# Gram and low-rank matmuls of two heads issued alternately on TensorE, in a one-core hybrid RWKV-7 / S5 / RG-LRU layer

## The chip, the cores and the metric

The kernel runs on one core of one Trainium2 chip. The metric is the device time of one execution in microseconds (us). Engines are named as in the profile: PE is TensorE (PEld its weight loads), DVE is VectorE, ACT is ScalarE, POOL is GpSimd, SP is the engine that issues the DMAs.

## What is computed

One layer (DEPTH is 1, 2048 frames, model width 1024, all float32). The input is normalised and projected to 4224 columns; three groups of 512 columns (RWKV-7, S5, RG-LRU) are mixed in time, gated, projected back and added; then comes a gated per-layer embedding and a final norm. The change lies in the RWKV-7 group, whose recurrence per head of width 64 is:

```
z = z + mu * (z_prev - z)
r, k, v, wd, ad = jnp.split(z, [...])
w = -jax.nn.softplus(-(w0 + jnp.tanh(wd) @ w2)) - 0.5          # low-rank matmul 1
a = jax.nn.sigmoid(a0 + ad @ a2)                               # low-rank matmul 2
kk = heads(k * k_k); kk = kk / max(norm(kk), 1e-12)
k = k * (1.0 + (a - 1.0) * k_a); b_h = kk * a_h; decay = exp(-exp(w))
def step(S, inp):
    S = S * d_t - (S kk_t) b_t^T + v_t k_t^T
    return S, S r_t
```

The reference steps frame by frame. The kernel does it in chunks of 64 frames: within a chunk all products of (b, k) of one frame with (kk, r) of another are needed, weighted with the decays between them. These are the Gram matrices of a chunk and a head: a 128 x 128 product with a contraction over the head's 64 channels.

## The kernel before, in words

The program has three parts in time. The mixers run to about 1143 us: the input projection (function `fills`, matmuls of lines 332 to 334, 128x512, three for each of eight slices, since the float32 product is split in a high and a low part) interleaved with the RWKV-7 work. After them come S5 with an output projection, and at the end the gated embedding and the final norm. The change touches the first part only.

RWKV-7 work is cut into 16 units: two head pairs and 256 frames each. A head pair fills the 128 partitions, head h = 0 on partitions 0 to 63 and head h = 1 on 64 to 127; the 512 columns of a unit's tiles are two pairs by 256 frames, or 8 chunks of 64 (index c). Each unit passes three stages, which run beside each other for successive units:

- *front* (`rwkv_front`): the two low-rank matmuls (line 396 into the PSUM tile `ps`, from partitions 0 to 63 of `zl`; line 398 into `psa`, from partitions 64 to 127), one each for the unit's two head pairs `hp`; from `ps` come `s`, its running sum `psl` (line 404) and the decays `ep`, `einv`; from `psa` comes `ta`. Then `kx` (kk and r, times decay) and `bk` (b and k, over decay) are made. Last come the Gram matmuls (line 461), in two halves of four chunks (`half_c`). For each half and each head there are four matmuls, lhsT = `bk` and rhs = `kx`, both on that head's 64 partitions, into one PSUM tile of 512 columns. That tile is then read by two ACT copies into `mt` (line 466) and two DVE multiplications with a mask into `kx` and `gr` (line 468, shown by the profile as line 80, the helper).
- *solve* (`rwkv_solve`): DVE inverts 32 x 32 blocks taken from `mt`: a transpose into `ms` (line 478) and 31 steps of a multiply and a subtract (`stmp`, `xs`, lines 487 and 489); PE completes the 64 x 64 inverses (lines 530 and 541), makes the bonus sums (line 511 into `psq`, read by DVE into `bon`) and transposes keys and values.
- *chain* (`rwkv_chain`): the state goes from chunk to chunk, PE matmuls of lines 570 to 603 between small DVE and ACT steps.

The order on PE is written out: the loop at line 883 takes steps of the projections and of the three stages by a credit, counted in matmuls, and under `manual_schedule` PE keeps exactly that order. The order on DVE, ACT and of the DMA issues on SP is set by the scheduler of the framework, by priorities and its own estimate of when each instruction can run. So a change of PE's order can also move instructions on the other engines.

The PSUM tiles of the front are taken from a ring of two banks named `prep`:

```
def pprep():
    return psum.tile([P, 512], F32, tag="prep", name="ps_prep", bufs=2)
```

In order of the program the ring serves `ps`, `psa`, `psn` (line 418), then head 0 and head 1 of the first Gram half, head 0 and head 1 of the second, and `psq` of a solve in between; each waits until the last reader of the tile two places before is done.

Each of these float32 matmuls is two entries in the profile: the 256 Gram matmuls of the program are 512 PE entries of line 461.

## Time and profile before

| what | value |
|---|---|
| timed runs | 1842.55, 1842.67, 1846.06 us (median 1842.67) |
| span of the profiled execution | 1844.3 us (the profile gives no other time for it) |
| PE busy, whole span | 1758.3 us, 95% |
| DVE busy, whole span | 1316.9 us, 71% |
| ACT busy, whole span | 928.6 us, 50% |
| stretch 60 to 1143 us (mixers) | PE busy 1054.91 of 1083 us, DVE 823.38, ACT 647.31 |
| Gram matmuls, line 461 | 512 entries, 55.8 us busy, 284 ns mean |
| low-rank matmuls, lines 396 and 398 | 64 entries each, 18.0 and 18.9 us busy |
| granted PE clock | 0.986 of full speed over the span |

How to read it: busy time of PE adds up entries that may overlap, and the ends of matmuls are modelled, so what a block of matmuls costs is read from the start of its first entry to the start of the next block, not from the sum of durations. The chain of waits follows the work that ended last back through the program: at each step to what released an instruction, or to the one before it on its engine. Work that isn't on that chain can get faster without the end moving.

### The profile page before, as it was taken

What the parts mean: (1) busy time and instruction counts of PE and PEld (TensorE: products, weight loads), DVE (VectorE), ACT (ScalarE), POOL (GpSimd) and SP (SyncE); (2) the same over time, 40 slices, a digit from 0 to 9 for tenths busy, and PEclk for the clock granted to TensorE, in tenths of its full rate; (3) what the DMA queues carried; (4) which work ended last, traced back from release to release, by engine and by line L of the source; (5) the groups of instructions that cost most, each with busy time, mean ns of one, the idle gap of its engine ahead of it and who ended that gap; (6) DMA issues with size and microseconds to landing.
All of it is one profiled execution on the core that took longest, in us unless ns stands there. A gap on an engine that the chain in (4) does not pass through costs nothing.

```text
span 1844.3 us, 30269 instructions
## 1 busy us (share of the span) xinstructions
PE 1758.3 (95%) x11244; PEld 1355.6 (74%) x11244; DVE 1316.9 (71%) x3301; ACT 928.6 (50%) x1797; POOL 39.8 (2%) x101
## 2 busy tenths in 40 slices
PE   5999999999998999999999999799999999999997
PEld 4877777777676777677776677577778878888886
DVE  6279788787986349898787875789996674455444
ACT  5345864575757444765557657433442443222222
POOL 1000000000000000000000000000000000000000
PEclk9999999999999999999999999899999999999999
DMA  4332322222223232223222122743435992122110
GB/s 145 120 111 68 97 90 85 90 60 76 83 78 103 92 123 76 66 90 106 80 76 66 53 60 87 193 147 102 121 121 165 254 293 82 65 70 76 58 46 35
DMA packets 214621, 184.72 MB, mean 100 GB/s; under 512 B 59253, under 2 KB 182474, under 8 KB 214474
## 3 DMA queue, kind: packets, MB, share of 16 engines
q1 hardware_dynamic: 214474, 182.79, 32.6%
q8 instruction: 89, 1.46, 0.3%
q14 instruction: 58, 0.48, 0.1%
HBM read 121.73 MB, written 59.83 MB: 98 GB/s over the span
## 4 chain that ended last, share of the span: by engine, by line
PE 64%; DVE 21%; ACT 8%; issue 4%; DMA 2%; POOL 0%; SPq 0%; POOLq 0%; ACTq 0%; DVEq 0%
PE ps_mm L332 9%; PE ps_mm L333 8%; PE ps_mm L334 8%; PE ps_mm L924 7%; PE ps_mm L922 7%; PE ps_mm L923 7%; DVE xs L80 3%; DVE stmp L80 3%; PE ps_prep L461 2%; ACT L101 1%; DVE w L80 1%; DVE ms L478 1%; PE ps_prep L1208 1%; PE ps_chain L570 1%; PE ps_prep L319 1%
## 5 line engine op out<-in xcount | busy, mean ns | idle before, releaser
L332 PE MATMUL ps_mm<-xh,whi 128*128 128x512 f32 x1056 | 462.9, 438 | 0.9 <-ACT whi L192 0.7
L333 PE MATMUL ps_mm<-xh,wlo 128*128 128x512 f32 x1056 | 415.9, 394 | 0.8 <-DVE wlo L80 0.8
L334 PE MATMUL ps_mm<-xl,whi 128*128 128x512 f32 x1056 | 416.0, 394 | 0.0
L332 PEld LDWEIGHTS ps_mm<-xh,whi 128*128 128x128 f32 x1056 | 199.8, 189 | 79.0 <-issue 31.2
L333 PEld LDWEIGHTS ps_mm<-xh,wlo 128*128 128x128 f32 x1056 | 200.4, 190 | 46.8 <-issue 13.1
L334 PEld LDWEIGHTS ps_mm<-xl,whi 128*128 128x128 f32 x1056 | 199.7, 189 | 45.3
L922 PE MATMUL ps_mm<-woh,yh 128*128 128x512 f32 x256 | 103.6, 406 | 12.2 <-ACT yh L101 12.2
L80 DVE TENSOR_TENSOR stmp<-xs,ms 128x60 f32<-128x60 f32 (+24 forms) x496 | 103.6, 209 | 11.6
L80 DVE TENSOR_TENSOR xs<-xs,stmp 128x60 f32<-128x60 f32 (+24 forms) x496 | 102.9, 207 | 11.5
L98 DVE SCALAR_TENSOR_TENSOR e<-ftg,e 128x1024 f32<-128x1024 f32 x16 | 19.6, 1226 | 118.6 <-ACT ftg L101 118.6
L923 PE MATMUL ps_mm<-woh,yl 128*128 128x512 f32 x256 | 102.8, 402 | 0.2 <-DVE yl L98 0.2
L924 PE MATMUL ps_mm<-wol,yh 128*128 128x512 f32 x256 | 103.0, 402 | 0.0
L924 PE MATMUL ps_mm<-pgl,hh 128*128 128x512 f32 x256 | 101.0, 395 | 0.0
L923 PE MATMUL ps_mm<-pgh,hl 128*128 128x512 f32 x256 | 100.9, 394 | 0.0
L922 PE MATMUL ps_mm<-pgh,hh 128*128 128x512 f32 x256 | 100.8, 394 | 0.0
L80 DVE TENSOR_TENSOR wlo<-wraw,whi 128x512 fp32r<-128x512 f32 x132 | 88.5, 684 | 14.9 <-ACT whi L192 14.5
L101 ACT ACT_TABLE_LOAD x70 | 89.8, 1283 | 12.2 <-DVE cs L80 11.0
L101 ACT ACTIVATE ftg<-ps_mm 128x512 f32<-128x512 f32 x32 | 19.1, 598 | 136.7 <-PE ps_mm L924 136.7
L98 DVE SCALAR_TENSOR_TENSOR z<-ps_mm,pc,z 128x511 f32<-128x511 f32 x48 | 35.8, 745 | 68.9 <-ACT z L101 68.8
L192 ACT CAST whi<-wraw 128x512 fp32r<-128x512 f32 x132 | 77.9, 614 | 0.9 <-DMA wraw<-in_w_in 0.5
L101 ACT ACTIVATE uv<-ps_chain 64x128 f32<-64x128 f32 x64 | 17.4, 272 | 97.3 <-DVE uv L93 96.7
L101 ACT ACTIVATE z<-ps_mm,dc 128x512 f32<-128x512 f32 x48 | 32.8, 682 | 65.4 <-PE ps_mm L334 65.2
(331 smaller groups left out, 3554.8 us busy)
## 6 DMA issues: line engine op xcount, KB each, us to landing
wraw<-in_w_in SPq DMA_DIRECT2D x132, 256.0 KB
zd<-z SPq DMA_DIRECT2D x48, 256.0 KB
yr<-Yd SPq DMA_DIRECT2D x16, 512.0 KB
ht<-in_x SPq DMA_DIRECT2D x16, 512.0 KB
Hd<-ht SPq DMA_DIRECT2D x16, 512.0 KB
hr<-Hd SPq DMA_DIRECT2D x16, 512.0 KB
out<-e SPq DMA_DIRECT2D x16, 512.0 KB
st<-in_w_out SPq DMA_DIRECT2D x12, 512.0 KB
```

The source lines that it names most:

```text
L80: V.tensor_tensor(out=out, in0=a, in1=b, op=op)
L98: V.scalar_tensor_tensor(out=out, in0=a, scalar=s, in1=b, op0=op0, op1=op1)
L101: A.activation(out=out, in_=in_, func=func, scale=scale, bias=bias)
L192: A.copy(out=hi[:, ks], in_=raw)
L319: T.transpose(out=ps[:, q * P:(q + 1) * P], in_=row[q][k // 4][:, k % 4 * P:(k % 4 + 1) * P], identity=ident)
L332: T.matmul(out=ps, lhsT=hi[:, k], rhs=xh, start=(k == 0), stop=False)
L333: T.matmul(out=ps, lhsT=lo[:, k], rhs=xh, start=False, stop=False)
L334: T.matmul(out=ps, lhsT=hi[:, k], rhs=xl, start=False, stop=(k == KD - 1))
L461: T.matmul(out=ps[:, q * P:(q + 1) * P], lhsT=bk[hs, c].rearrange("p a t -> p (a t)"), rhs=kx[hs, c, h:3:2 - h], start=True, stop=True)
L922: T.matmul(out=ps, lhsT=a_h[:, k], rhs=b_h[k][:, ns], start=(k == 0), stop=False)
L923: T.matmul(out=ps, lhsT=a_l[:, k], rhs=b_h[k][:, ns], start=False, stop=False)
L924: T.matmul(out=ps, lhsT=a_h[:, k], rhs=b_l[k][:, ns], start=False, stop=(k == nk - 1))
```

## The change

The two heads' Gram matmuls of a half are issued in turn: chunk by chunk, first head 0, then head 1, each head still into a PSUM tile of its own. Both tiles are therefore taken from the ring before the first matmul, and the readers (ACT copies, DVE multiplications) of both heads stand behind all eight matmuls in the program. The two low-rank matmuls are issued in turn likewise, for each head pair one of each. The number of instructions, their operands and the PSUM tiles stay as they were. Comment lines are removed too, which shifts line numbers by one or so: in the changed kernel the low-rank matmuls are lines 396 and 397, the Gram matmul is line 460.

```diff
         for hp, cs in hps:
             T.matmul(out=ps[:, cs], lhsT=wla[0:64, hp * P:(hp + 1) * P], rhs=zl[0:64], start=True, stop=True)
-        for hp, cs in hps:
             T.matmul(out=psa[:, cs], lhsT=wla[64:128, hp * P:(hp + 1) * P], rhs=zl[64:128], start=True, stop=True)
...
         for half_c in range(2):
             yield 1
             cs = slice(4 * half_c, 4 * half_c + 4)
+            pair_ps = [pprep(), pprep()]
+
+            for q in range(4):
+                c = 4 * half_c + q
+                for h in range(2):
+                    hs = slice(64 * h, 64 * h + 64)
+                    T.matmul(out=pair_ps[h][:, q * P:(q + 1) * P], lhsT=bk[hs, c].rearrange("p a t -> p (a t)"),
+                             rhs=kx[hs, c, h:3:2 - h], start=True, stop=True)
             for h in range(2):
                 os = slice(64 * (1 - h), 64 * (1 - h) + 64)
-                ps = pprep()
-                for q in range(4):
-                    c = 4 * half_c + q
-                    hs = slice(64 * h, 64 * h + 64)
-                    T.matmul(out=ps[:, q * P:(q + 1) * P], lhsT=bk[hs, c].rearrange("p a t -> p (a t)"),
-                             rhs=kx[hs, c, h:3:2 - h], start=True, stop=True)
-                psq4 = ps.rearrange("p (c t) -> p c t", t=P)
+                psq4 = pair_ps[h].rearrange("p (c t) -> p c t", t=P)
                 for bl in range(2):
                     g = slice(64 * h + 32 * bl, 64 * h + 32 * bl + 32)
                     A.copy(out=mt[g, cs, 0:C - 32 * bl], in_=psq4[g, :, 32 * bl:C])
```

On PE, at the Gram matmuls of the first unit's first half: `ps_prep_1063` is head 0's PSUM tile, `ps_prep_1072` (before) and `ps_prep_1064` (after) head 1's; `x4` means four matmuls in a row. Before:

```order
L334 MATMUL ps_mm_1042<-xl_478,whi_867 128x512
L461 MATMUL ps_prep_1063<-kx_978,bk_988 128x128 x4
L461 MATMUL ps_prep_1072<-kx_978,bk_988 128x128 x4
L332 MATMUL ps_mm_1042<-xh_489,whi_867 128x512
L333 MATMUL ps_mm_1042<-xh_489,wlo_868 128x512
```

Now:

```order
L460 MATMUL ps_prep_1063<-kx_978,bk_988 128x128
L460 MATMUL ps_prep_1064<-kx_978,bk_988 128x128
L460 MATMUL ps_prep_1063<-kx_978,bk_988 128x128
L460 MATMUL ps_prep_1064<-kx_978,bk_988 128x128
L460 MATMUL ps_prep_1063<-kx_978,bk_988 128x128
L460 MATMUL ps_prep_1064<-kx_978,bk_988 128x128
L460 MATMUL ps_prep_1063<-kx_978,bk_988 128x128
L460 MATMUL ps_prep_1064<-kx_978,bk_988 128x128
```

The four of head 1 moved up between those of head 0; the projections around them stand as before. The same holds for all 32 such blocks.

On PE, at the low-rank matmuls of the first unit (`ps_prep_936` is `ps`, `ps_prep_937` is `psa`), before:

```order
L334 MATMUL ps_mm_915<-xl_466,whi_795 128x512
L396 MATMUL ps_prep_936<-zl_892,wla_242 128x256 x2
L398 MATMUL ps_prep_937<-zl_892,wla_242 128x256 x2
L332 MATMUL ps_mm_915<-xh_477,whi_795 128x512
L333 MATMUL ps_mm_915<-xh_477,wlo_796 128x512
```

Now:

```order
L396 MATMUL ps_prep_936<-zl_892,wla_242 128x256
L397 MATMUL ps_prep_937<-zl_892,wla_242 128x256
L396 MATMUL ps_prep_936<-zl_892,wla_242 128x256
L397 MATMUL ps_prep_937<-zl_892,wla_242 128x256
L332 MATMUL ps_mm_915<-xh_477,whi_795 128x512
```

The second head pair's matmul into `ps` now stands behind the first one into `psa`. Apart from these two kinds of block PE's order is the same from end to end.

On DVE the instructions are the same ones, but their order moved. At the eighth unit's running sum `psl`, which stands among the seventh unit's solve steps (`stmp`, `xs`) and chain steps (`sp`, `uv`), before:

```order
L80 TENSOR_TENSOR stmp<-xs,ms 128x2x27
L404 SCALAR_TENSOR_TENSOR psl<-cmask,s 128x512
L80 TENSOR_TENSOR xs<-xs,stmp 128x2x27
L80 TENSOR_TENSOR stmp<-xs,ms 128x2x26
L80 TENSOR_TENSOR xs<-xs,stmp 128x2x26
L98 SCALAR_TENSOR_TENSOR lth<-lr,lth 128x512
```

Now:

```order
L80 TENSOR_TENSOR xs<-xs,stmp 128x4x16
L80 TENSOR_TENSOR wlo<-wraw,whi 128x512
L80 TENSOR_TENSOR stmp<-xs,ms 128x5x15
L692 COPY lru_h<-lr 128x1
L403 SCALAR_TENSOR_TENSOR psl<-cmask,s 128x512
L80 TENSOR_TENSOR xs<-xs,stmp 128x5x15
```

`psl` moved back by 36 instructions, from the solve step of width 27 to that of width 15. It is the largest move on DVE: of its 3303 instructions 992 stand at another place than before, 798 of these by at most four places. ACT has 70 loads of function tables instead of 71.

## The prediction

> **What bounds the kernel now.** I read the page first, then the busy times by stretch, then the chain of waits, then single blocks on the timeline.

> ```profile
> span 1844.3 us, 30269 instructions
> PE 1758.3 (95%) x11244; PEld 1355.6 (74%) x11244; DVE 1316.9 (71%) x3301; ACT 928.6 (50%) x1797; POOL 39.8 (2%) x101
> PE 64%; DVE 21%; ACT 8%; issue 4%; DMA 2%; POOL 0%; SPq 0%; POOLq 0%; ACTq 0%; DVEq 0%
> 60.00:1143.00 1083.00, 1054.91 (x8099) 784.49 (x8098) 823.38 (x2392) 647.31 (x1313) 12.96 (x36) 0.99 0.28 83
> ```

> The third line is the chain's share by engine; the last is the mixers' stretch (length, then busy time of PE, PEld, DVE, ACT, POOL). PE is almost never idle there, 28 us of 1083, and looks like the bound. But DVE is busy for 823 us (76%), and a fifth of the chain is DVE's. So PE and DVE take turns in setting the end, and what PE saves counts only where the chain runs over PE. Everything that is changed lies in this stretch; the later 701 us stay.

> **What a Gram block costs.** One block (half a unit, both heads) on the PE timeline: start, time from the first start to the last end, line, shape, number of entries.

> ```profile
> 113.28 1.71 PE L461 MATMUL ps_prep<-kx,bk 64*128 64x128 f32 x16
> 114.92 0.50 PE L332 MATMUL ps_mm<-xh,whi 128*128 128x512 f32 x1
> ...
> 1057.26 1.16 PE L461 MATMUL ps_prep<-kx,bk 64*128 64x128 f32 x8
> 1060.94 1.13 PE L461 MATMUL ps_prep<-kx,bk 64*128 64x128 f32 x8 [2.53 <-DVE gr L80]
> ```

> The last two rows are lucky: in this one block head 1 had to wait for its PSUM bank, so each head stands alone. A head alone takes 1.16 or 1.13 us; both in a row take 1.71, not 2.3. So they overlap already, with head 1 starting about 1.71 - 1.16 = 0.55 us after head 0. If they started together the block would take 1.16 and a bit. Whether they can is shown by two other blocks, which have the wanted order or act like it:

> ```profile
> 99.25 0.48 PE L396 MATMUL ps_prep<-zl,wla 64*128 64x256 f32 x1
> 99.26 0.48 PE L398 MATMUL ps_prep<-zl,wla 64*128 64x256 f32 x1
> ...
> 100.00 0.38 PE L396 MATMUL ps_prep<-zl,wla 64*128 64x256 f32 x1
> 100.01 0.38 PE L398 MATMUL ps_prep<-zl,wla 64*128 64x256 f32 x1
> ...
> 129.72 1.15 PE L519 MATMUL ps_late<-cen,zv 64*64 64x64 f32 x32
> ...
> L519 PE MATMUL ps_late<-cen,zv 64*64 64x64 f32 x512 | 18.4, 221 | 0.7 <-ACT kb L506 0.7
> ```

> The low-rank matmuls of lines 396 and 398, on the two halves of the partitions as the Gram matmuls are, start 0.01 us apart from first to last, although all four entries of 396 stand ahead of those of 398 in the program. Line 519 alternates the heads already: 32 entries in 1.15 us, one of them 0.22 long (last row: the group's mean is 221 ns), so one every (1.15 - 0.22) / 31 = 0.03 us. PE can thus issue far faster than the 1.16 / 16 = 0.07 us that the alternated Gram block asks for, and a second stream on the other 64 partitions costs 0.01 us. My reading: PE looks ahead over a few entries only. Four of the other head are within reach (low rank), eight are not (Gram), and alternation puts the partner next in line.

> **The change, part by part.** *Gram.* New block: 1.16 + 0.01 = 1.17 us; saved 1.71 - 1.17 = 0.54 us per block. There are 512 entries / 16 = 32 blocks, so PE's own slots shrink by 32 x 0.54 = 17.3 us. The bounds of the saving per block are 0 (PE starts head 1 no earlier, for a reason that the rows don't show) and 0.55 (no offset at all); I take 0.54, since the low-rank pairs show it on the same row halves.

> *Low rank.* Worth 0 on PE where nothing waits: the pairs overlap to 0.01 us before. In a few units `psa` waits for its bank; the longest of these waits (the bracket is idle time and its releaser):

> ```profile
> 462.64 1.13 PE L396 MATMUL ps_prep<-zl,wla 64*128 64x256 f32 x4
> 465.26 2.04 PE L398 MATMUL ps_prep<-zl,wla 64*128 64x256 f32 x4 [1.50 <-DVE stmp L80]
> ```

> Head 1's rows start 2.62 us late here, for DVE has to free the bank. Now the second matmul into `ps` queues behind the waiting one, so `s` and the sum `psl` can start up to 2.6 us later than today. PE's own end stays: after the wait four entries of each stream run side by side at most, as four of 398 do today. The cover for the late `s` is the distance from here to the unit's Gram matmuls, which the chain's list puts at 512.67, 47 us later. So I cost it at 0; without that cover it would cost up to 2.6 us in this unit.

> *Readers.* The same ACT copies and DVE multiplications as before; head 0's results are ready at the same time after the block's start (1.16 us), head 1's 0.54 earlier. Nothing is added there. The wait that is new: head 1's bank is needed at the start of the block instead of 0.55 us into it, and all of head 0's matmuls but the first stand behind it.

> *What of 17.3 us lies on the chain.* The list of the longest pieces of the chain shows which Gram blocks set the end:

> ```profile
> 113.35 1.64 PE ps_prep L461 x16
> 157.79 1.85 PE ps_prep L461 x15
> 222.31 1.64 PE ps_prep L461 x16
> 226.63 1.10 PE ps_prep L461 x11
> ...
> 512.67 1.64 PE ps_prep L461 x16
> ...
> 682.67 1.89 PE ps_prep L461 x15
> ...
> 720.12 1.66 PE ps_prep L461 x15
> 724.84 1.78 PE ps_prep L461 x16
> ...
> 1003.47 1.64 PE ps_prep L461 x16
> 1007.76 1.10 PE ps_prep L461 x11
> 1060.94 1.13 PE ps_prep L461 x8
> ```

> Of 32 blocks, 28 are in it. Sixteen are whole and undisturbed (x16, 1.64 us; first 113.35, last 1003.47), and 720.12 is nearly that: 17 blocks. Seven (x11; first 226.63, last 1007.76) are left after 11 entries: the chain goes over to ACT when head 0 is ready, and head 0 gets no faster. Four (157.79, 682.67, 724.84, 1060.94) contain a wait for another engine. Four are off the chain. What follows an x11 block:

> ```profile
> 227.75 0.36 ACT mt L466
> ...
> 256.69 0.28 ACT uv L101
> ...
> 257.02 0.45 PE ps_chain L592 x8
> ```

> From 227.75 to 257.02 the end is set by ACT's copies, the solve on DVE and what DVE and ACT do between, and PE, busy all that time, joins again at line 592. If PE arrives there 0.54 us sooner, it waits 0.54 us longer. How close the two paths are is in the waits of PE in 60 to 1150 us (total, times, longest):

> ```profile
> PE ps_chain L592 <- ACT uv L101: 3.0, 6, 0.8
> ```

> Six waits of 0.8 us at most: the two paths have the same length within a microsecond. That is why I count the x11 and the off-chain blocks (11 x 0.54 = 5.9 us) at nothing. The four with waits I count at nothing as well; they are worth between 0 and 0.54 each.

> *Sum.* 17 x 0.54 = 9.2 us on the chain. Taking time off one path brings the other up at some of these 17 places too; I take 2 of them as lost (between 0 and 17; the six short waits say few), so 15 x 0.54 = 8.1 us. The profiled execution would go from 1844.3 to 1836.2. The median of the timed runs, 1842.7, lies 1.6 below that span, so I forecast 1842.7 - 8.1 = **1834.6 us**.

> *The reordered DVE and ACT.* The moves of 992 DVE instructions cost or gain what the trace of before can't show. A solve step is a pair of 0.2 us:

> ```profile
> L80 DVE TENSOR_TENSOR stmp<-xs,ms 128x60 f32<-128x60 f32 (+24 forms) x496 | 103.6, 209 | 11.6
> ```

> The largest move, 36 places, is worth at most about 36 x 0.2 = 7 us of delay for one `psl`, under the 47 us of cover; the moves of up to four places are worth 0.8 us each, with both signs. As a sum I take 0, with 4 us to either side (an estimate: five such moves that fall the same way and are met by a waiting PE). One load of a function table less on ACT is left at 0, ACT being busy for 647 of 1083 us.

> **The rivals.**

> *All of PE's saving counts (chance 0.17).* If DVE follows PE (its moved order lets the solves start sooner), all blocks but the four with waits pay: 28 x 0.54 = 15.1 us, 1827.6 us. For it: PE busy 97% of the stretch. Against it: the x11 blocks, and 29 us of DVE and ACT on end behind one of them.

> *The gain turns into waits for PSUM banks (chance 0.18).* Banks are freed by DVE, which isn't faster. Behind the second half of a unit the freeing stands late on DVE:

> ```profile
> 342.01 0.42 DVE L80 TENSOR_TENSOR gr<-ps_prep,gm 128x256 f32<-128x256 f32 x1
> 342.35 2.03 DVE L478 STREAM_TRANSPOSE ms<-mt 128x1024 f32<-128x1024 f32 x1
> ...
> 345.73 0.41 DVE L80 TENSOR_TENSOR gr<-ps_prep,gm 128x256 f32<-128x256 f32 x1
> ```

> Head 1's bank is free at 346.1, 3.7 us after head 0's at 342.4, because the transpose stands between. A PE that is ahead meets this at the next user of the ring, as it does today at 465.26. If it eats 12 or more of the 17, at most 5 x 0.54 = 2.7 us remain: 1840 to 1843, say 1841 us. Against it: at 222 to 227 and the like both halves run without a wait. [...]

> *Slower: DVE's new order makes PE wait (chance 0.10).* Chain steps (`sp`, `uv`) that now stand behind more solve steps come late, and PE, in written order, waits at line 592 in unit after unit. A move by four places costs 4 x 0.2 = 0.8 us; ten such waits that aren't there today (8.1 / 0.8) undo the forecast's gain, and from there on the time gets longer. With one in each of the 16 units it is 16 x 0.8 - 8.1 = 4.7 us slower, 1847.4 us. For it: DVE is 76% busy and a fifth of the chain. Against it: most moves are small and of both signs.

> *The change doesn't do what it says (chance 0.03).* If PE serialised entries whose partner has just started, blocks would stay at 1.71 and the time at 1842.7. The low-rank rows speak against it.

> **How the numbers follow.** Forecast 0.52, all counts 0.17, waits 0.18, no effect 0.03, slower 0.10. The likeliest case alone spans 1831 to 1839 (8.1 with 4 either way). The range takes in the full saving below and no saving above: 1827 to 1844; slower than 1844 and faster than 1827 together hold under 2 in 10. What a measurement of this kernel tells from no change is about 0.2%, 3.7 us, so faster means under 1839.0 and slower over 1846.4. Faster: all of the 0.17, 0.48 of the 0.52 and 0.05 of the waits, 0.70. Same: the forecast's edge (0.04), the rest of the waits and no effect (0.16), the mildest fifth of the slower case (0.02), 0.22. Slower: 0.08.

> **What would show it.** In the changed profile a Gram block of 16 entries reads 1.17 us instead of 1.71, with the next line-332 matmul 0.54 us sooner; if it reads 1.4 or more, the look-ahead step is wrong. Line 396 and its partner stay 0.01 us apart. PE's waits at 592 and 581 and for `prep` banks grow by some 6 to 9 us in total; if they grow by 15, the second rival holds, if by 2, the first. The mixers end (1143 us before) at about 1135; a move elsewhere, after 1143, would refute that the change works where I say.

## The result and the profile after

The change makes the kernel slower: 1859.58 us (median of four runs, 1856.73 to 1864.2) against 1843.05 (four runs, 1842.55 to 1846.06). The ratio is 1.0084, 95% interval 1.0066 to 1.0102. The forecast was 1834.6 with a range up to 1844, so sign and range are both wrong. One of the ten executions of run e7 (below) took 2446.71 us at a granted clock of 0.656; that run's median and ratio are of the other nine.

From the page of the changed kernel: span, busy times, the chain's share by engine; then the mixers' stretch from the busy times by stretch (length, PE, PEld, DVE, ACT, POOL busy, granted clock, DMA share and GB/s).

```profile
span 1862.5 us, 30258 instructions
PE 1758.8 (94%) x11244; PEld 1351.0 (73%) x11244; DVE 1321.6 (71%) x3301; ACT 928.0 (50%) x1796; POOL 39.9 (2%) x101
PE 56%; DVE 25%; ACT 10%; issue 4%; DMA 3%; POOL 0%; SPq 0%; POOLq 0%; ACTq 0%; DVEq 0%
60.00:1143.00 1083.00, 1035.48 (x7950) 765.57 (x7949) 816.65 (x2369) 630.75 (x1287) 13.05 (x36) 0.97 0.27 82
```

PE, DVE and ACT are less busy in this stretch, and fewer of their instructions fall into it (7950 of PE's entries instead of 8099). On the chain PE's share fell from 64% to 56%, and DVE's and ACT's together rose from 29% to 35%. PE's granted clock in the stretch fell from 0.99 to 0.97.

All of the loss lies in the mixers. The last `ps_y` matmuls of the mixers (line 603 before, 604 after; start, time, shape, entries), first before, then after:

```profile
1142.38 0.40 PE L603 MATMUL ps_y<-gr,uv 128*64 128x64 f32 x8
```

```profile
1162.04 0.40 PE L604 MATMUL ps_y<-gr,uv 128*64 128x64 f32 x8
```

The mixers end 19.66 us later; the span grew by 18.2. Yet the Gram block did get shorter, as wanted (timeline of PE, after):

```profile
224.44 1.16 PE L460 MATMUL ps_prep<-kx,bk 64*128 64x128 f32 x16
225.53 0.50 PE L332 MATMUL ps_mm<-xh,whi 128*128 128x512 f32 x1
```

From the block's start to the next line-332 matmul it is 1.09 us, where the undisturbed block of before at 113.28 has 114.92 - 113.28 = 1.64. What grew are PE's waits (after; 60 to 1170 us; total, times, longest):

```profile
PE ps_prep L460 <- DVE gr L80: 8.5, 4, 4.2
PE ps_prep L512 <- ACT nrow L419: 5.5, 1, 5.5
...
PE ps_prep L460 <- DVE bk L80: 5.2, 3, 2.4
PE ps_chain L593 <- ACT uv L101: 4.2, 7, 0.8
...
PE ps_prep L397 <- DVE stmp L80: 2.4, 1, 2.4
```

All of PE's rows of this view up to 1165 us add up to 47.1 us after and 27.6 before. The new ones are few and long.

**Where the time went.** PE runs the same `ps_y` matmuls in the same order in all kernels, so their starts can be subtracted. The table gives, for eleven of the 64 groups of line 603, how much later (+) each kernel starts them than the kernel before. All are taken from the timelines of PE, one profiled execution of each kernel; the runs are described below. The executions differ: that of e3 is the slowest of its ten (1852.74, median 1845.67), those of before and after are the slowest of four, that of e9 is the fastest of four. So a step counts here where several columns show it.

| start before, us | after | e5 | e9 | e10 | e6 | e3 | e2 | e1 | e4 | e7 |
|---|---|---|---|---|---|---|---|---|---|---|
| 257.30 | 1.5 | 0.9 | 0.7 | 1.1 | 0.4 | 1.1 | 0.6 | 0.8 | -1.3 | -1.2 |
| 371.28 | 3.4 | 5.5 | 3.7 | 1.2 | 0.4 | 1.1 | 1.9 | -0.4 | -1.2 | 1.6 |
| 402.58 | 8.5 | 5.5 | 3.7 | 1.2 | 0.4 | 7.4 | 8.0 | -0.5 | -1.8 | 1.6 |
| 472.85 | 5.7 | 3.9 | 2.0 | -0.1 | 0.3 | 4.7 | 2.7 | -2.6 | -8.7 | -4.8 |
| 497.74 | 12.2 | 11.0 | 8.9 | 1.8 | 0.4 | 4.6 | 4.4 | -2.6 | -9.2 | -5.7 |
| 611.68 | 11.9 | 10.3 | 8.2 | 1.2 | 2.4 | 4.5 | 4.8 | -3.2 | -7.7 | -4.8 |
| 738.31 | 14.9 | 13.5 | 11.4 | 2.9 | 0.8 | 7.9 | 5.9 | -4.8 | -9.1 | -2.9 |
| 784.96 | 14.1 | 12.5 | 10.4 | 2.0 | 0.9 | 7.4 | 5.1 | -4.8 | -9.1 | 1.3 |
| 796.67 | 18.6 | 14.8 | 12.7 | 2.0 | 0.9 | 7.4 | 5.1 | -4.8 | -5.8 | 1.3 |
| 926.84 | 16.6 | 14.6 | 12.5 | 2.1 | 0.9 | 4.6 | 4.2 | -5.5 | -7.9 | 2.7 |
| 1142.38 | 19.7 | 14.4 | 14.0 | 5.0 | 0.9 | 5.9 | 6.2 | -2.9 | -10.7 | 1.5 |

The kernel after loses in a few steps: 5.1 us between 371 and 403, 6.5 between 473 and 498, 3.0 between 612 and 738, 4.5 between 785 and 797. In between the figure falls, by 0.55 us at an undisturbed Gram block and where the kernel before loses time itself, as at 465 us. Two of the steps were followed down to their cause. In each of the other two PE waits at a Gram block for DVE's `bk` (2.44 us at 733.44, 2.06 us at 801.51); why `bk` is late there stays open.

**The step at 473 to 498 us: the running sum comes late.** After, on ACT, DVE and PE:

```profile
472.84 0.84 ACT L101 ACTIVATE s<-ps_prep,dc 128x256 f32<-128x256 f32 x2
...
482.25 0.62 ACT L101 ACTIVATE s<-s 128x512 f32<-128x512 f32 x1
...
486.00 1.22 DVE L403 TENSOR_TENSOR_SCAN psl<-cmask,s 128x512 f32<-128x512 f32 x1
...
487.25 0.63 ACT L101 ACTIVATE ep<-psl 128x512 f32<-128x512 f32 x1 [2.87 <-DVE psl L403]
...
488.67 0.56 ACT L419 COPY nrow<-ps_prep 2x512 f32<-2x512 f32 x1
...
489.28 2.07 PE L512 MATMUL ps_prep<-zr,blk 128*128 128x512 f32 x2 [5.52 <-ACT nrow L419]
```

Before:

```profile
464.31 0.84 ACT L101 ACTIVATE s<-ps_prep,dc 128x256 f32<-128x256 f32 x2
...
465.65 0.62 ACT L101 ACTIVATE s<-s 128x512 f32<-128x512 f32 x1
...
466.50 1.22 DVE L404 TENSOR_TENSOR_SCAN psl<-cmask,s 128x512 f32<-128x512 f32 x1
...
479.28 0.56 ACT L420 COPY nrow<-ps_prep 2x512 f32<-2x512 f32 x1
...
479.89 1.12 PE L511 MATMUL ps_prep<-zr,blk 128*128 128x512 f32 x2 [1.87 <-ACT nrow L420]
```

Before, ACT's two steps on `s` stand almost side by side and `psl` starts 2.19 us after the first of them. After, ACT does ten other instructions between them (two table loads, steps of other groups, copies, casts), some of them after waits of their own, and `psl` starts 13.16 us after the first. `s` is ready at 482.87 (482.25 + 0.62); the last 3.1 us up to 486.00 are DVE's own order. `psl` stands 19.5 us later than before, while the PE matmuls around it stand 5.7 later. Behind `psl`, in ACT's order, come `ep`, `einv`, `ta` and then `nrow`, the copy that empties `psn`, and PE's line 512 (`psq`) waits for that copy: 5.52 us.

**The step at 371 to 403 us: the Gram readers are split.** After (the first half's block is at 389, the second's here):

```profile
391.40 1.01 ACT L467 COPY mt<-ps_prep 32x256 f32<-32x256 f32 x3
392.13 0.43 DVE L80 TENSOR_TENSOR kx<-ps_prep,gm 64x256 f32<-64x256 f32 x1
392.44 0.72 ACT L101 ACTIVATE lth<-lr,dc 128x512 f32<-128x512 f32 x1
392.57 0.42 DVE L80 TENSOR_TENSOR gr<-ps_prep,gm 128x256 f32<-128x256 f32 x1
...
393.61 0.48 PE L460 MATMUL ps_prep<-kx,bk 64*128 64x128 f32 x2
...
396.55 0.26 ACT L467 COPY mt<-ps_prep 32x128 f32<-32x128 f32 x1
396.81 0.69 DVE L98 SCALAR_TENSOR_TENSOR lth<-lr,lth 128x512 f32<-128x512 f32 x1
...
397.75 0.41 DVE L80 TENSOR_TENSOR gr<-ps_prep,gm 128x256 f32<-128x256 f32 x1
398.30 1.69 PE L460 MATMUL ps_prep<-kx,bk 64*128 64x128 f32 x14 [4.21 <-DVE gr L80]
```

Before:

```profile
388.01 1.29 ACT L466 COPY mt<-ps_prep 32x256 f32<-32x256 f32 x4
...
389.85 0.41 DVE L80 TENSOR_TENSOR gr<-ps_prep,gm 128x256 f32<-128x256 f32 x1
...
390.75 1.71 PE L461 MATMUL ps_prep<-kx,bk 64*128 64x128 f32 x16
```

Before, the first half's four ACT copies stand in one run and head 1's `gr` ends at 390.26, before PE needs the bank. After, ACT's fourth copy stands 4.1 us after the start of the work put ahead of it (396.55 - 392.44). On DVE head 0's `gr` is done at 393.0, but `li`, `g`, two splits `wlo` and `lth` stand before head 1's `kx` and `gr`, two of them behind waits for ACT (0.91 and 0.41 us). Head 1's `gr` is the last reader and ends at 398.16. The second half's block stops after two entries (one matmul of head 0), since head 1's bank is not free until then.

### The profile page after: what moved, and what is told of

It is laid out like the page before. It is cut to its first block, busy times and chain, and to the rows that moved or that the text cites. A ratio compares the mean times of both kernels' runs of the same rounds, so it can differ in the third digit from the quotient of the medians.

```text
span 1862.5 us, 30258 instructions
## 1 busy us (share of the span) xinstructions
PE 1758.8 (94%) x11244; PEld 1351.0 (73%) x11244; DVE 1321.6 (71%) x3301; ACT 928.0 (50%) x1796; POOL 39.9 (2%) x101
## 4 chain that ended last, share of the span: by engine, by line
PE 56%; DVE 25%; ACT 10%; issue 4%; DMA 3%; POOL 0%; SPq 0%; POOLq 0%; ACTq 0%; DVEq 0%
PE ps_mm L332 8%; PE ps_mm L925 7%; PE ps_mm L923 7%; PE ps_mm L924 7%; PE ps_mm L333 7%; PE ps_mm L334 7%; DVE xs L80 4%; DVE stmp L80 3%; ACT L101 2%; PE ps_prep L460 2%; DVE w L80 1%; DVE ms L479 1%; DVE wlo L80 1%; ACT rst L101 1%; PE ps_prep L319 1%
## 5 line engine op out<-in xcount | busy, mean ns | idle before, releaser
L332 PE MATMUL ps_mm<-xh,whi 128*128 128x512 f32 x1056 | 467.7, 443 | 2.0 <-ACT la L101 1.3
L332 PEld LDWEIGHTS ps_mm<-xh,whi 128*128 128x128 f32 x1056 | 202.3, 192 | 81.5 <-issue 32.6
L923 PE MATMUL ps_mm<-woh,yh 128*128 128x512 f32 x256 | 103.7, 406 | 11.4 <-ACT yh L101 11.4
L80 DVE TENSOR_TENSOR xs<-xs,stmp 128x60 f32<-128x60 f32 (+24 forms) x496 | 103.3, 208 | 12.3
L80 DVE TENSOR_TENSOR stmp<-xs,ms 128x60 f32<-128x60 f32 (+24 forms) x496 | 103.4, 208 | 11.7
L80 DVE TENSOR_TENSOR wlo<-wraw,whi 128x512 fp32r<-128x512 f32 x132 | 88.6, 684 | 12.2 <-ACT whi L192 11.8
L101 ACT ACT_TABLE_LOAD x69 | 88.5, 1283 | 12.2 <-DVE cs L80 11.0
L101 ACT ACTIVATE ftg<-ps_mm 128x512 f32<-128x512 f32 x32 | 19.1, 598 | 137.5 <-PE ps_mm L925 137.5
L101 ACT ACTIVATE z<-ps_mm,dc 128x512 f32<-128x512 f32 x48 | 32.8, 682 | 64.7 <-PE ps_mm L334 64.6
L923 PEld LDWEIGHTS ps_mm<-woh,yh 128*128 128x128 f32 x256 | 48.8, 191 | 21.4 <-ACT yh L101 11.8
```

Of the source, the lines that this page charges most:

```text
L80: V.tensor_tensor(out=out, in0=a, in1=b, op=op)
L101: A.activation(out=out, in_=in_, func=func, scale=scale, bias=bias)
L332: T.matmul(out=ps, lhsT=hi[:, k], rhs=xh, start=(k == 0), stop=False)
L923: T.matmul(out=ps, lhsT=a_h[:, k], rhs=b_h[k][:, ns], start=(k == 0), stop=False)
```

## The experiments

Two kinds of thing differ between the two kernels: PE's order, which is written out, and the order on ACT, DVE and SP, which the scheduler makes anew from the changed program. Two theories were set against each other: PE's new order itself causes the waits (banks are needed sooner), or the other engines' new order does. The runs cut the change along both lines: Gram part or low-rank part, PE's order or the others' order. Ratios are to the kernel before, run beside it on the same chip, with their 95% intervals.

### One half of the change at a time: e3 and e5

e3 is the Gram part alone, so without this line of the diff; e5 is this line alone:

```diff
-        for hp, cs in hps:
             T.matmul(out=psa[:, cs], lhsT=wla[64:128, hp * P:(hp + 1) * P], rhs=zl[64:128], start=True, stop=True)
```

> Only the Gram matmuls in turn, the low-rank ones as before. Both theories: all of the loss is in the Gram part, 1856 to 1862. If the low-rank part carries it (one matmul into ps queued behind the wait for psa's bank), 1838 to 1846.

> Only the low-rank matmuls in turn, the Gram matmuls head by head as before. Theory C: the second matmul into ps, now behind the one that waits for psa's bank, makes s, psl and in the end the copy nrow late, and nrow holds the bank that line 511 needs; this made most of the change's loss: 1848 to 1857, with a wait of 3 us or more at line 511 or 398 near 480 us. Rival: the low-rank part costs nothing by itself, and the loss of the change beyond the Gram part comes from both edits meeting in one order of the engines: 1842 to 1846.

e3: 1845.67 us, 1.0009 (0.9995 to 1.0024). e5: 1859.21, 1.0090 (1.0065 to 1.0115). The part that I had costed at nothing carries the whole loss, and the part that was to gain gains nothing. e3 shows the step at 371 to 403 us in the table, not the one at 473 to 498; e5 the reverse. e3 lies outside the 1856 to 1862 of both theories, in the range set down for a loss by the low-rank part. e5 lies above the range of its theory C and has the long wait that was named there (5.51 us at line 510); the queue that theory C gives as the reason is what e6 takes apart.

### The low-rank part: PE's order or the others' order: e6 and e9

In e6 only PE's low-rank matmuls are reordered in the finished program of before; ACT, DVE and SP keep their order. e9 is the opposite: the finished program of e5, with PE's low-rank matmuls put back to the order of before.

```diff
 PE, each low-rank block, e6 against before (e9 against e5 is the reverse)
-396 hp0, 396 hp1, 398 hp0, 398 hp1
+396 hp0, 398 hp0, 396 hp1, 398 hp1
```

> The low-rank matmuls in turn on TensorE only; all other engines keep the order of the kernel before, instruction by instruction. If the queueing behind psa's wait itself is the cost, it is still there: s comes up to 2.6 us late in four units, and ACT, which keeps its order, waits for it: 1846 to 1852. If the scheduler's new order is the cost, nothing remains: 1842 to 1846.

> DVE, ACT and the DMA issues in the order that the scheduler makes for the low-rank matmuls in turn, but TensorE runs them head by head as before (Gram as before too). If the new order of the engines is the whole cost of the low-rank edit: 1852 to 1862. If order and queueing on TensorE are both needed: 1842 to 1848.

e6: 1846.24 us, 1.0006 (0.9992 to 1.0021), and in the table never more than 2.4 us from before. e9: 1858.58, 1.0080 (1.0062 to 1.0098), as slow as e5 with the intervals overlapping. So PE's order of the low-rank matmuls costs nothing that can be measured, and the loss comes with the order that the scheduler made on the other engines for it. The queueing that theory C names is there in e6: `psl` of the eighth unit starts at 468.94, 2.4 us later than before. But the wait for `nrow` is 1.95 us, hardly more than the 1.87 of before. At the place of the late sum, e9:

```profile
470.28 0.84 ACT L101 ACTIVATE s<-ps_prep,dc 128x256 f32<-128x256 f32 x2
478.54 0.63 ACT L101 ACTIVATE s<-s 128x512 f32<-128x512 f32 x1
485.57 2.07 PE L510 MATMUL ps_prep<-zr,blk 128*128 128x512 f32 x2 [5.50 <-ACT nrow L419]
```

PE runs the low-rank matmuls here as before, and still the two steps on `s` are 8.3 us apart and PE waits 5.50 us.

### Is it this place? e10

e10 is e5 with four results moved forward in the scheduler's eyes, in all 16 units:

```diff
+        with tc.high_priority(offset=100):
             ... the three steps that make s and psl
+        with tc.high_priority(offset=100):
             ... the step that makes ta
+        with tc.high_priority(offset=100):
             A.copy(out=nrow[0:2], in_=psn[0:2])
```

> The low-rank matmuls in turn as in the run of that edit alone (1859.2), and the steps behind them (the ACT steps into s, the running sum psl on DVE, ta, nrow) get a priority 100 higher in the scheduler. In the eighth unit the step that finishes s then stands 11 ACT instructions earlier and psl 21 DVE instructions earlier. Theory D, the late s and psl of that unit make nrow late, and line 511's matmul waits 5.5 us for nrow's bank: that wait falls to 2 us or less and the time to 1843 to 1853. If the loss is spread over many other moves: 1855 or more.

1850.32 us, 1.0031 (1.0016 to 1.0047): the loss is 0.31% instead of e5's 0.90%, and the intervals don't overlap; at the end of the mixers it is 5.0 us instead of 14.4. In e10:

```profile
468.16 0.84 ACT L101 ACTIVATE s<-ps_prep,dc 128x256 f32<-128x256 f32 x2
470.85 0.62 ACT L101 ACTIVATE s<-s 128x512 f32<-128x512 f32 x1
...
479.98 1.47 PE L513 MATMUL ps_prep<-zr,blk 128*128 128x512 f32 x2 [2.02 <-ACT nrow L422]
```

The wait for `nrow` is back to 2.0 us, and the step from 473 to 498 shrank from 7.1 us (e5) to 1.9. The other large difference is between 257 and 371 us, 4.6 us in e5 and 0.1 here. In e5 PE waits there for ACT's `stmp`, a step of the solve:

```profile
272.86 0.69 PE L540 MATMUL ps_late<-tm,stmp 32*32 32x32 f32 x32 [1.37 <-ACT stmp L534]
```

Behind it the granted clock is 0.50 from 273.9 to 280.6 us, and the matmuls of lines 333 and 334 at 276.75 start 0.43 us apart. e10 has neither the wait (0.16 us at 271.81) nor the lower clock (the same two at 274.41 start 0.23 us apart). Why `stmp` is late in e5 stays open, and what is left of the loss isn't explained piece by piece.

### The Gram part: PE's order or the others' order: e1 and e2

The same cut. e1: the finished program of before, with PE's Gram matmuls in turn. The last of the 32 blocks stays head by head, because in the old order of the other engines head 1's bank is released there by work that stands behind head 0's readers. e2: the program with the Gram part alternated, and with PE's Gram matmuls put back head by head.

```diff
 PE, each Gram block, e1 against before (e2 is the reverse, with the new order elsewhere)
-h0 c0, h0 c1, h0 c2, h0 c3, h1 c0, h1 c1, h1 c2, h1 c3
+h0 c0, h1 c0, h0 c1, h1 c1, h0 c2, h1 c2, h0 c3, h1 c3
```

> The Gram matmuls of the two heads in turn on TensorE, as in the change, but DVE, ACT and the DMA issues keep the order of the kernel before, instruction by instruction (the low-rank matmuls stay as before, and the very last of the 32 blocks stays head by head, because with the old order head 1's PSUM bank is only freed there after head 0's results are read). Theory A, the new order of DVE and ACT costs the time: blocks of 1.16 us and 1830 to 1838 us, the gain that was forecast. Theory B, the alternation itself costs it, because a block now needs both heads' PSUM banks and both heads' inputs at its first matmul: waits at the Gram blocks grow by 15 us or more and the time is 1850 to 1860.

> The reverse: DVE, ACT and the DMA issues in the order that the scheduler makes for the alternated Gram matmuls, but TensorE runs the Gram matmuls head by head as before. Theory A: as slow as the change or slower, since the bad order is there and the shorter blocks are not: 1858 to 1870. Theory B: about as before, 1840 to 1848.

e1: 1841.05 us, 0.9991 (0.9981 to 1.0001). e2: 1850.44, 1.0026 (1.0012 to 1.0040). The new order alone costs 0.26%. Neither came out as set down: e1 lies above theory A's range and below theory B's, e2 above theory B's and below theory A's. The block that waited 4.21 us after, now in e1 and then in e2:

```profile
389.84 1.32 PE L461 MATMUL ps_prep<-kx,bk 64*128 64x128 f32 x16
```

```profile
396.85 2.04 PE L461 MATMUL ps_prep<-kx,bk 64*128 64x128 f32 x8 [3.00 <-DVE gr L80]
```

With the old order of readers the alternated block runs through in 1.32 us; with the new one even head 1 alone waits 3.00 us. The step at 371 to 403 belongs to the order of the readers, not to that on PE. But with the old order the alternation is worth only 2.9 us at the end of the mixers, and the interval of the timed runs just reaches no change.

### Keeping the readers together: e4, e7, e8, e12

```diff
                 psq4 = pair_ps[h].rearrange("p (c t) -> p c t", t=P)
+                with tc.high_priority(offset=100):
                     for bl in range(2):
                         ... the two ACT copies into mt, the two DVE multiplications into kx and gr
```

e4 is the Gram part with this, e12 the same with an offset of 60, e8 the whole change with it, and e7 the kernel before (no alternation) with it.

> Gram matmuls in turn, and the readers of the Gram tiles (the ACT copies into mt, the DVE multiplications into kx and gr) get a priority 100 higher in the scheduler, so that in its order no other ACT or DVE work stands between the readers of head 0 and those of head 1. Theory A, in the form that late readers of head 1 hold TensorE: 1830 to 1842. Theory B: still 1850 or more. If the order hurts elsewhere than at these readers: 1846 to 1858.

> The kernel before with the raised priority of the Gram readers alone, no alternation. If the priority alone made the gain of the kernel that has both: 1832 to 1837. If the two add up (banks come free earlier, and blocks are 0.55 us shorter): 1837 to 1843.

> The whole change, with the raised priority of the Gram readers. Theory C: the low-rank part still costs what it costs, 8 to 12 us over the 1834.5 of the kernel with only the Gram matmuls in turn: 1840 to 1848. If late Gram readers were all of it: 1832 to 1838.

> Gram matmuls in turn with the Gram readers' priority raised by 60 instead of 100; head 1's readers stand at most two DVE instructions behind head 0's. If the place of these readers is what counts: 1832 to 1838, as with 100. If the 100 run only had a lucky order: 1840 or more.

| run | median, us | ratio to before |
|---|---|---|
| e4, Gram part, readers raised by 100 | 1834.46 | 0.9946 (0.9929 to 0.9963) |
| e12, the same by 60 | 1838.21 | 0.9967 (0.9956 to 0.9978) |
| e7, before, readers raised by 100 | 1845.84 | 1.0007 (0.9997 to 1.0018) |
| e8, whole change, readers raised by 100 | 1841.91 | 0.9979 (0.9963 to 0.9995) |

Raising the readers alone gives nothing that can be measured and neither does alternating alone (e1, e3); e4 with both gains half a per cent, e12 a third. e4 and e8 lie in a range set down for them; e7 lies above both of its ranges, and e12 just above the one for "as with 100". e4 is the fastest kernel found. Its mixers end here:

```profile
1131.72 0.40 PE L606 MATMUL ps_y<-gr,uv 128*64 128x64 f32 x8
```

That is 10.7 us before the kernel before, and 12.2 before e7 by the table. The gain isn't made of Gram blocks alone: 6.9 of the 10.7 us come between 453 and 473 us (-1.8 at the group that starts at 452.61 before, -8.7 at 472.85), where the kernel before waits 1.50 us at line 398 for `psa`'s bank and e4 doesn't. The granted clock there is 0.50 from 465.1 to 471.9 us before, and 1.00 from 458 to 472 in e4. The low-rank matmuls there, e4:

```profile
459.70 0.48 PE L396 MATMUL ps_prep<-zl,wla 64*128 64x256 f32 x1
459.72 0.48 PE L398 MATMUL ps_prep<-zl,wla 64*128 64x256 f32 x1
```

e7 gains at that place as well (-4.8) and loses it later (+1.3 at 785 us). So 12.2 us is the worth of the alternation in one order against another order, not a clean count of blocks.

e8 is 7.4 us slower than e4, near the 8 to 12 expected, but not at the late sum: `psl` of the eighth unit starts at 468.68 there, 0.2 us behind `s`, the wait for `nrow` is 1.09 us, and the step at 473 to 498 us is gone. The mixers of e8 end 5.3 us later than those of e4, and 5.2 of these are there by 319 us, behind a wait of 2.24 us for ACT's `stmp` at 272.33, the place where e5 waits too.

### All priorities together: e11

e11 is e4 with the raised `s`, `psl`, `ta` and `nrow` of e10 as well, and with `bon`, the reader of `psq`, raised by 60; the low-rank matmuls stay as before.

> The Gram matmuls in turn, the low-rank ones as before, and a higher priority for all readers of the two prep banks: the Gram readers, s, psl, ta, nrow (100) and bon (60). If freeing the banks early is what lets the shorter blocks pay: 1826 to 1834. If the moved front work delays the chain in return: 1835 to 1845.

1838.63 us, 0.9973 (0.9961 to 0.9985), no better than e4. The intervals of the two just overlap, so whether e11 is slower at all stays open. The profiled spans, 1833.3 and 1833.6 us, don't decide it, since e11's profile is of the fastest of its ten executions. The time lies in the range set down for moved front work that delays the chain; no run shows that this is the reason.

## Why the prediction was wrong

**The size of a Gram block: right.** 1.17 us were forecast and 1.16 measured, in 22 of the 32 blocks; the next matmul comes 0.55 us sooner (1.09 instead of 1.64). This agrees with the look-ahead reading; how many entries PE looks ahead over was my estimate, and no run varies it.

**Low rank on PE: right, and beside the point.** The reordered matmuls alone (e6) change nothing measurable. The delay of `psl` by up to 2.6 us is there (2.4) and is covered, as forecast.

**The late `s` under "47 us of cover": the step that failed first.** I let the delay of `s` and `psl` run against the unit's Gram matmuls at 512.67. But other work stands behind `psl` in ACT's written order: `ep`, `einv`, `ta`, then `nrow`, for which PE's line 511 waits. The profile of before already had the row, 1.87 us of waiting at 479.89 for `nrow`. The cover for anything that delays `nrow` was therefore below nothing. `psl` itself, done at 467.72, had 2.2 us to `ep` (469.93) and 10.2 to `einv` (477.91), not 47. The 2.4 us that come from PE's order (e6) move `ep` by only 0.7 us; the far larger delay that the new order on ACT and DVE brought reached `nrow`. I followed the data (what reads `psl`) and not the queue (what is written behind its readers).

**"The reordered DVE and ACT: 0, with 4 us to either side": the term that was mis-sized.** It is worth 1.008 in e9, where the low-rank part's order acts alone (14.0 us at the end of the mixers), and 1.0026 in e2, where the Gram part's does (6.2 us). No run pairs the order of the whole change with PE's order of before. The largest move that I listed, `psl` back by 36 places, is the one at 486.00. I priced a place at a solve step of 0.2 us, 7 us in all. It stands 13.8 us later than the matmuls around it (19.5 less 5.7): the work between is also a scan of 1.28, splits of 0.69 and a wait of 2.34 us, and the delay begins on ACT, whose order I hadn't priced at all.

**Readers, "nothing is added there": wrong.** The same instructions in another order kept a bank full: 4.21 us at 398.30. What I named as the new wait (head 1's bank needed at the block's start) is the right wait, but what made it long is the split of the readers. e1 and e2 separate the two.

**What of 17.3 us lies on the chain: not settled.** I counted 15 of 32 blocks. e1 keeps 2.9 us, e4 against e7 12.2 us, that is 5 and 23 blocks; how many count depends on the order of the other engines. The table in the part on the clock says how: the blocks get shorter in each of these runs, and part of it comes back as PE's waits and as time at a lower clock.

**The rivals.** The slower one, DVE's new order making PE wait (chance 0.10), had the right agent and sign. Its place was wrong: PE's waits at line 593 grew from 3.0 to 4.2 us, not by 0.8 in each unit. Its price was 4.7 us where the mixers lost 19.7; few long waits did it, not one short wait per unit. PSUM banks did eat a gain in e3, as the second rival said, but by the readers' order rather than because DVE isn't faster.

**The signs that I had named.** The block's time came as said. PE's waits grew by 19.5 us; 6 to 9 were forecast, and 15 were set down for the second rival. The mixers end at 1162, not at 1135.

**A term that was missing: the clock.** Behind the wait of 5.52 us, after, the matmuls are slow:

```profile
493.28 0.63 PE L333 MATMUL ps_mm<-xh,wlo 128*128 128x512 f32 x1
493.71 0.63 PE L334 MATMUL ps_mm<-xl,whi 128*128 128x512 f32 x1
```

The same two of before, behind a wait of 1.87 us:

```profile
481.94 0.39 PE L333 MATMUL ps_mm<-xh,wlo 128*128 128x512 f32 x1
482.17 0.39 PE L334 MATMUL ps_mm<-xl,whi 128*128 128x512 f32 x1
```

They start 0.43 us apart instead of 0.23, and line 512 itself took 2.07 us for 1.12. The granted clock there is 0.50 (489.28 to 493.20 us), against 1.00 before (479.80 to 483.00). Over the whole span it fell from 0.986 to 0.977.

What this costs can be estimated from the traces. The figures above say what to take: at a granted clock of 0.50 two matmuls started 0.43 us apart for 0.23, and line 512 took 2.07 us for 1.12, so about half of the time in which PE is busy at 0.50 is counted as lost. From 60 us to the end of the mixers that is 8.9 us before and 26.9 after. The table sets it beside PE's waits and the Gram saving (0.54 us for each alternated block). All figures are us against the kernel before; the last column is the last row of the table of starts.

| run | Gram saving | PE's waits | lower clock | sum | measured |
|---|---|---|---|---|---|
| after | -17.3 | 19.5 | 18.0 | 20.2 | 19.7 |
| e9 | 0 | 9.5 | 5.2 | 14.7 | 14.0 |
| e2 | 0 | 1.4 | 4.8 | 6.2 | 6.2 |
| e3 | -17.3 | 10.0 | 11.4 | 4.1 | 5.9 |
| e1 | -16.7 | 7.3 | 3.9 | -5.5 | -2.9 |
| e4 | -17.3 | 6.8 | -2.3 | -12.8 | -10.7 |

The sums come within 3 us of what was measured, so by this estimate the lower clock costs the changed kernel about as much as the waits themselves (18.0 and 19.5 us). The table also limits what e4 shows. PE waits as long in its mixers as in those of e1 (34.4 and 34.9 us); what e4 has less of is time at half clock (13.7 us against 27.3). That split readers hold PE up is shown for the step at 371 to 403 us; that keeping them together is the reason for the whole of e4's gain is not shown.

## What to carry to other kernels

Where a scheduler sets the order on some engines, a reordering on another engine is two changes: build the two apart (the new order there with the old one here, and the reverse) before believing a cost for either. Price a moved instruction not by who reads its result but by what stands behind its readers in their queues, and look for a row in which somebody already waits for the last of these: there the cover is gone. Here a faster producer into a ring of two PSUM banks stopped where the readers of the two banks were split (4.21 us at 398.30), so look at their order before counting the gain. And the wait of 5.52 us on TensorE cost more than its own length: behind it the matmuls started 0.43 us apart instead of 0.23, at a granted clock of 0.50, so look at what follows a long wait as well.

## What the runs showed of the hardware

In the kernel before, PE did not start the matmuls on the two row halves in their written order. Of the four low-rank entries of line 396 the last starts at 100.00, 0.74 us after the first of line 398 at 99.26, although all four stand ahead of it. With eight entries ahead (a Gram block) the other half starts 0.55 us late: in the block at 113.28 the sixteen starts make two rows of eight with the same spacing (0.21 us, then about 0.11), one from 113.28 and one from 113.83. Read as head 0's and head 1's, head 1's first entry starts right behind the fifth of head 0 (113.82) and ahead of its last three.

In the kernel before, the wait of 1.50 us at 465.26 is followed by a 2.04 us block of line 398 (granted clock 0.50), where the block of line 396 ahead of the wait takes 1.13 (granted clock 1.00), while after the wait of 1.87 us at 479.89 line 511 keeps its 1.12 (granted clock 1.00).
